# A decoder trunk in float32: the first feed-forward product by Strassen's seven, with stage pools that share bytes

## The chip, the cores and the metric

The kernel runs on one core of one Trainium2 chip. The metric is the device time of one execution in microseconds (us). Times of one kernel are given as a median of runs; a trace is one profiled execution.

## The reference

Two layers over x of 512 tokens by 1024 channels, all in float32. In each layer four causal token mixers read h = RMSNorm(x) @ W_in, and then:

```
mixed = sum_i sigmoid(gate_logits_i + b_gate_i) * (y_i @ W_branch_i)
x  <- x + mixed @ W_out
h2 = rms_norm(x, norm_ff)
x  <- x + square(relu(h2 @ W_ff1)) @ W_ff2
```

W_ff1 is 1024 x 4096 and W_ff2 is 4096 x 1024. A last RMSNorm ends it. The change concerns the part from `mixed @ W_out` on.

## The kernel before, in words

Activations lie transposed: tiles of 128 channels by 512 tokens, eight of them (x0 to x7) for x. Each float32 operand is split in two float32r tiles, a high part (a ScalarE copy) and the rest (a VectorE subtraction), and a product is made of three matmuls: high x high, low x high and high x low. Weights come in pieces of 128 x 1024 float32 (512 KB) from one array in the order of use. `chunk` (L265) issues the DMA of a piece (L271) from SyncE's queue into one of three buffers (wr0, wr1, wr2, a ring), copies the high part into a tile wh (L275, ScalarE) and leaves the low part in the buffer itself (L276, VectorE), so that a buffer is free only when the last matmul that reads its low part is done. `mtile` (L279) makes one tile of 128 output channels: 8 pieces of the contraction with 3 matmuls each, 24 of 128x512.

`layer` (L419) does the attention part as a list of steps written by hand, and ends it with the four branch products. Then come 8 tiles of w_out (L463), each added to x on VectorE; `norm_split` (L363) scales x by g and splits it into hh and hl; `rms` (L328) makes 1/rms by squares (ScalarE), additions (GpSimd, L339), a matmul with ones, a power (GpSimd) and a broadcast matmul. The feed-forward part has 4 groups: 8 tiles of w_ff1 (L472), each written out by max(0, .) * 1/rms (L475), squared (L476) and split (L478, L479), and 8 tiles of w_ff2 (L484), added to x (L485). `final` (L381) squares x, sums, and writes the scaled tiles out; the last w_ff2 tile is made in two halves of the tokens (`mhalves`, L291).

All tiles come from one pool `sb`, each tag with its own bytes for the whole program; the rings wr (3 of 1024 columns), yl and e (6 each of 512) are buffers laid out by hand. The Tile framework orders the instructions of each engine by priorities that the code sets (`high_priority`), and puts semaphore waits where a tile is read or its bytes reused. An engine takes its instructions strictly in that order, and so does SyncE's DMA queue.

## Time and profile before

| what | value |
|---|---|
| time, median of 3 runs | 2278.67 us (2275.55, 2278.67, 2278.78) |
| span of the profiled execution | 2273.7 us |
| median of the runs less that span | 5.0 us |
| TensorE busy | 98% of the span, 10740 matmuls, 10740 weight loads |
| VectorE, ScalarE, GpSimd busy | 65%, 46%, 19% |
| DMA | 204.75 MB, 90 GB/s on average |

The span goes from the first to the last record of the trace; the device time holds a little more at both ends. Busy is the sum of an engine's own instructions; the chain of waits goes back from the last instruction to what released it, step by step. "Granted clock" is the share of full speed that TensorE was given in a stretch: 1.00 is 2.4 GHz, 0.50 is 1.2 GHz.

### The profile page before, as it was taken

The page shows a single profiled execution, that of the slowest core. Times are in us where ns is not written, and L with a number is a line of the kernel's source. Part 1 is how long each engine was busy: PE and PEld are TensorE (multiplying, and loading weights), DVE is VectorE, ACT ScalarE, POOL GpSimd, SP SyncE. Part 2 cuts the span into 40 slices and gives each one's busy share as a digit, 9 for nine tenths or more (in the row PEclk, how much of TensorE's full clock was granted, in tenths as well). Part 3 has the DMA queues.
Part 4 walks back from the last instruction along what each step waited for, and adds up shares of the span by engine and source line. Part 5 has one row for each costly group of instructions (what it writes and reads, how often), then busy time and mean ns, then how long its engine had stood idle before and what let it go on. Part 6 is the DMA issues. An engine that isn't in the chain of part 4 may idle for free.

```text
span 2273.7 us, 28986 instructions
## 1 busy us (share of the span) xinstructions
PE 2230.2 (98%) x10740; PEld 1824.9 (80%) x10740; DVE 1488.2 (65%) x2434; ACT 1035.6 (46%) x1663; POOL 428.5 (19%) x759
## 2 busy tenths in 40 slices
PE   8999999999899999999999999999989999999998
PEld 7888878887788888888888888788868888888886
DVE  6889687888875444343458886978888654344344
ACT  5775544445544333232347654534454443232233
POOL 1223024434211200000112220234431112000000
PEclk9999999999999999999999999999999999999999
DMA  4222223322124332333432222233211243333332
GB/s 164 77 72 68 90 68 96 113 79 79 47 67 128 103 93 93 95 99 94 125 105 69 66 75 85 74 98 118 76 56 58 83 130 93 94 99 95 93 94 92
DMA packets 63108, 204.75 MB, mean 90 GB/s; under 512 B 7496, under 2 KB 10184, under 8 KB 62968
## 3 DMA queue, kind: packets, MB, share of 16 engines
q1 hardware_dynamic: 62968, 202.90, 29.1%
q8 instruction: 86, 1.41, 0.3%
q14 instruction: 54, 0.44, 0.1%
HBM read 198.57 MB, written 4.29 MB: 89 GB/s over the span
## 4 chain that ended last, share of the span: by engine, by line
PE 91%; DVE 5%; issue 1%; DMA 1%; ACT 1%; POOL 1%; POOLq 0%; DVEq 0%; SPq 0%; ACTq 0%
PE ps L121 48%; PE pd L121 42%; PE ps L730 1%; DMA wr1f<-in_w 0%; DMA wr0f<-in_w 0%; DVE sh L844 0%; POOL sm L613 0%; DVE wr1r L276 0%; DVE Q L616 0%; DVE m L1214 0%; DVE m L591 0%; DVE sx L609 0%; DVE m L605 0%; DVE Q L1109 0%; ACT wh L275 0%
## 5 line engine op out<-in xcount | busy, mean ns | idle before, releaser
L121 PE MATMUL pd<-hh,wh 128*128 128x512 f32 x1040 | 415.8, 400 | 0.2 <-ACT wh L275 0.2
L121 PE MATMUL pd<-hl,wh 128*128 128x512 f32 x1040 | 407.8, 392 | 0.0
L275 ACT ACTIVATE wh<-wr1f 128x1024 fp32r<-128x1024 f32 x112 | 118.7, 1060 | 274.7 <-PE ps L121 175.0
L275 ACT ACTIVATE wh<-wr0f 128x1024 fp32r<-128x1024 f32 x111 | 117.6, 1060 | 265.4 <-PE ps L121 176.3
L121 PEld LDWEIGHTS pd<-hh,wh 128*128 128x128 f32 x1040 | 195.6, 188 | 50.0 <-issue 4.0
L275 ACT ACTIVATE wh<-wr2f 128x1024 fp32r<-128x1024 f32 x111 | 117.6, 1060 | 256.9 <-PE ps L121 172.7
L121 PEld LDWEIGHTS pd<-hl,wh 128*128 128x128 f32 x1040 | 195.5, 188 | 42.2 <-issue 0.5
L121 PE MATMUL ps<-hh,wh 128*128 128x512 f32 x512 | 201.3, 394 | 0.0
L121 PE MATMUL ps<-hl,wh 128*128 128x512 f32 x512 | 199.3, 389 | 0.0
L276 DVE TENSOR_TENSOR wr0r<-wr0f,wh 128x1024 fp32r<-128x1024 f32 x111 | 143.4, 1292 | 43.0 <-ACT wh L275 42.5
L485 DVE TENSOR_TENSOR x<-x,ps 128x512 f32<-128x512 f32 (+1 forms) x65 | 44.2, 679 | 191.7 <-PE ps L121 191.7
L276 DVE TENSOR_TENSOR wr2r<-wr2f,wh 128x1024 fp32r<-128x1024 f32 x111 | 144.5, 1302 | 35.0 <-ACT wh L275 34.8
L121 PE MATMUL pd<-hh,wr2r 128*128 128x512 f32 x392 | 156.6, 400 | 0.0
L276 DVE TENSOR_TENSOR wr1r<-wr1f,wh 128x1024 fp32r<-128x1024 f32 x112 | 138.1, 1233 | 28.2 <-ACT wh L275 27.7
L475 DVE SCALAR_TENSOR_TENSOR p<-ps,rb 128x512 f32<-128x512 f32 x64 | 43.9, 691 | 157.3 <-PE ps L121 149.2
L121 PE MATMUL ps<-v,wh 128*128 128x512 f32 (+1 forms) x392 | 135.8, 389 | 0.0
L121 PE MATMUL pd<-hh,wr1r 128*128 128x512 f32 x336 | 134.4, 400 | 0.0
L121 PE MATMUL pd<-hh,wr0r 128*128 128x512 f32 x312 | 124.6, 399 | 0.0
L121 PE MATMUL ps<-p,v 128*128 128x384 f32 (+3 forms) x384 | 116.1, 426 | 2.2 <-POOL p L633 2.2
L121 PEld LDWEIGHTS ps<-hh,wh 128*128 128x128 f32 x512 | 96.1, 188 | 24.6 <-issue 0.5
L121 PE MATMUL pd<-yh,wh 128*128 128x512 f32 x256 | 105.0, 410 | 9.9 <-ACT yh L492 9.0
L121 PEld LDWEIGHTS ps<-hl,wh 128*128 128x128 f32 x512 | 96.2, 188 | 21.3
(638 smaller groups left out, 5326.8 us busy)
## 6 DMA issues: line engine op xcount, KB each, us to landing
wr0f<-in_w SPq DMA_DIRECT2D x117, 512.0 KB, 3.6
wr1f<-in_w SPq DMA_DIRECT2D x117, 512.0 KB, 3.6
wr2f<-in_w SPq DMA_DIRECT2D x116, 512.0 KB, 3.6
G<-gd SPq DMA_DIRECT2D x48, 128.0 KB, 3.1
x<-in_x SPq DMA_DIRECT2D x16, 256.0 KB, 3.5
xs<-x SPq DMA_DIRECT2D x8, 256.0 KB, 3.7
x<-xs SPq DMA_DIRECT2D x8, 256.0 KB, 3.3
out_y<-p SPq DMA_DIRECT2D x8, 256.0 KB, 2.4
```

Of the source, the lines that this page charges most:

```text
L121: i = self.nc.tensor.matmul(o, l, r, start=start, stop=stop, skip_group_check=True)
L275: nc.scalar.activation(wh[:], raw.f[:], AF.Copy)
L276: nc.vector.tensor_sub(raw[:], raw.f[:], fb(wh[:]))
L475: nc.vector.scalar_tensor_tensor(r[:], o[:], 0.0, self.rb[:], OP.max, OP.mult)
L485: nc.vector.tensor_add(x[m][:, h], x[m][:, h], o[:])
L730: nc.tensor.transpose(S3[n][:, c:c + P], at(F, q)[:, j * P:(j + 1) * P], self.ident)
```

## The change

The four groups of w_ff1 tiles become eight blocks of 512 hidden channels. For each, the 1024 x 512 piece of W_ff1 is seen as 2 x 2 quarters of 512 x 256, and x (scaled by g) as 2 x 2 quarters of 512 channels x 256 tokens. Winograd's form of Strassen's method makes the four quarter outputs of seven products instead of eight. `product` makes one of them with 24 matmuls of 128x256. The combinations of x (seven factors F11, F21, F22, F1 to F4, each high and low) are made once per layer in `factors`; those of the weights (s1 to s4) per block in `quarters`, by four VectorE additions of 128x1024 on the raw quarters; all seven weights of a block are split. Outputs are put together on the way out of PSUM: X, Y and Z are PSUM banks, `taken` copies one that goes on accumulating (e1, e2, e3). `finish` makes the last two products of a block, after product 11 of the next one. A w_ff2 group (`down`) stands after the blocks 2, 4 and 6 and at the end, there with `finish` between the two halves of its first two tiles' contraction.

The norm's scaling moves: the relu's and the square's results stay unscaled, x is multiplied by the mean square at the first block (8 VectorE multiplications) and by its reciprocal when the last w_ff2 group is added. `square_norm` makes both, so there are two broadcast matmuls per layer for one.

Storage: attention, feed-forward and end each open a pool of their own, and pools of different stages share bytes; a tile waits for the last reader of the bytes below it. In the feed-forward part the rings wr, yl and e together are nine buffers of 1024 columns (wr0 to wr2 and ww3 to ww8, of which ww3 to ww5 lie over yl and ww6 to ww8 over e), handed out by `take` in order of a list and given back by `drop`. wh has 5 buffers there instead of 2.

The core of the diff:

```
+    FF = dict(wh=(5, 1024), fx=(8, 1024), rl=(3, 1024), m=(2, 512), p=(6, 512), rt=(2, 4), ms=(2, 512))
+    END = dict(m=(1, 512), p=(4, 512), r=(3, 256), rt=(2, 4))
+    def stage(self, name, tags):
+        self.tags = tags
+        pool = self.tc.tile_pool(name=name, bufs=1, reuse_waits="tile")
...
+        nw = self.DUAL["wr"][0]
+        self.wfree = self.ring["wr"][1] + [pair("ww", i, 1024, start + i * 4096) for i in range(nw, total // 4096)]
+    def take(self):
+        b = self.wfree.pop(0)
...
+    def drop(self, d):
+        d.live = False
+        self.wfree.append(d.home)
...
             for l in range(self.depth):
-                x = self.layer(l, x)
-            self.final(x)
+                with self.stage(f"att{l}", self.ATT):
+                    self.mix(l, x)
+                with self.stage(f"ff{l}", self.FF):
+                    x = self.feed(l)
+            with self.stage("end", self.END):
+                self.final(x)
...
+        for m in OUT_ORDER:
+            wh, wl = self.chunk(wide=True)
+            o = self.ps("d")
+            self.halves(wh, wl, X2(HH), X2(HL), o[:], range(KT))
+            self.drop(wl)
...
+        for n in range(8):
+            W = self.quarters()
+            s = dict(W=W, X=self.ps("s"), H=hid)
+            self.product(s["X"], W["11"], F["11"], True)
+            s["e1"] = self.taken(s["X"])
+            if pend:
+                self.finish(pend, F)
+            if n > 0 and n % 2 == 0:
+                self.down(x, hid[:4], None)
+                del hid[:4]
+            if n == 0:
+                for k in range(KT):
+                    nc.vector.tensor_mul(x[k][:], x[k][:], ms[:])
+                s["Z"] = self.ps("s")
+                self.product(s["Z"], W["12"], F["21"], True)
+            s["Y"] = self.ps("s")
+            self.product(s["Y"], W["s3"], F["3"], True)
+            self.product(s["X"], W["s2"], F["2"], False)
+            s["e2"] = self.taken(s["X"])
...
+            self.product(s["X"], W["s1"], F["1"], False)
+            with self.evac():
+                e3 = self.taken(s["Y"])
+                nc.vector.tensor_add(s["rb"][:, S:], s["X"][:], e3[:])
+            pend = s
+        self.down(x, hid, rs, pend, F, l == self.depth - 1)
...
+    def product(self, o, W, F, start):
+        (wh, wl), (fh, fl) = W, F
+        for m in range(2):
+            d = o[:, m * 256:m * 256 + 256]
+            for k in range(4):
+                s = slice(k * 256 + m * P, k * 256 + m * P + P)
+                t = slice(k * 256, k * 256 + 256)
+                self.mm(d, wh[:, s], fh[:, t], start and m == 0 and k == 0, False)
+                self.mm(d, wl[:, s], fh[:, t], False, False)
+                self.mm(d, wh[:, s], fl[:, t], False, k == 3)
+        self.drop(wl)
+    def quarters(self):
+        with self.tc.high_priority(2000):
+            q = {}
+            for n in QUARTERS:
+                q[n] = self.take()
+                nc.sync.dma_start(q[n].f[:], self.A["w"][self.cidx])
+                self.cidx += 1
+            for d, a, b in (("s1", "21", "22"), ("s3", "21", "11"), ("s2", "s1", "11"), ("s4", "s2", "12")):
+                q[d] = q["21"] if d == "s3" else self.take()
+                nc.vector.tensor_add(q[d].f[:], q[a].f[:], q[b].f[:])
+            out = {}
+            for n in ("11", "s3", "s2", "12", "s1", "s4", "22"):
+                wh = self.t("wh", 1024, F32R)
+                nc.scalar.activation(wh[:], q[n].f[:], AF.Copy)
+                nc.vector.tensor_sub(q[n][:], q[n].f[:], fb(wh[:]))
...
+    def finish(self, s, F):
+        self.product(s["X"], W["s4"], F["22"], False)
+        with self.evac():
+            nc.scalar.activation(s["ra"][:, S:], s["X"][:], AF.Relu)
+            self.squares(s["ra"], s["H"], 1.0)
+        self.product(s["Y"], W["22"], F["4"], False)
+        with self.evac():
+            nc.vector.tensor_add(s["rb"][:, 0:S], s["Y"][:], s["e2"][:])
+            nc.scalar.activation(s["rb"][:], s["rb"][:], AF.Relu, scale=-1.0)
+            self.squares(s["rb"], s["H"], 1.0)
...
+                    nc.vector.tensor_add(x[m][:, h], x[m][:, h], o[:, 0:h.stop - h.start])
+                    if rs is not None:
+                        nc.vector.tensor_mul(x[m][:, h], x[m][:, h], rs[:, h])
...
+OUT_ORDER = (0, 1, 4, 5, 2, 3, 6, 7)
+QUARTERS = ("21", "22", "11", "12")
```

Three places show how the order moves. The first is SyncE's DMA queue in layer 0 around the end of the branches, before (line L271 is a weight, L160 a tile of x). The first w_out tile reads the wr1 of the fourth row, and the last branch tile the wr0 of the first.

```order
L271 DMA wr0f_55<-in_w 128x1024
L160 DMA x4_6601<-in_x 128x512
L160 DMA x5_6603<-in_x 128x512
L271 DMA wr1f_57<-in_w 128x1024
L271 DMA wr2f_59<-in_w 128x1024
L271 DMA wr0f_55<-in_w 128x1024
L160 DMA x6_6605<-in_x 128x512
L160 DMA x7_6607<-in_x 128x512
```

The same place now (L301 a weight, L577 a raw quarter, L190 a tile of x). The last branch tile reads the wr0 of the first row.

```order
L301 DMA wr0f_55<-in_w 128x1024
L301 DMA wr1f_57<-in_w 128x1024
L301 DMA wr2f_59<-in_w 128x1024
L301 DMA ww6f_91<-in_w 128x1024
L301 DMA ww7f_93<-in_w 128x1024
L301 DMA wr0f_55<-in_w 128x1024
L577 DMA ww8f_95<-in_w 128x1024
L190 DMA x0_6604<-in_x 128x512
```

The first w_out tile now takes the second wr0, of the sixth row, and the second and third tiles the wr1 and wr2 ahead of it; the seventh and eighth tiles take ww6 and ww7. All tiles of x stand behind them.

The second place is VectorE in layer 0 around the end of a w_ff2 group that is not the last, before: x6 and x7 are the last additions (L485), wr0r to wr2r low parts of weights (L276), L475 and L479 the work on a w_ff1 tile.

```order
L276 TENSOR_TENSOR wr1r_58<-wr1f_57,wh_1031_7934 128x1024
L485 TENSOR_TENSOR x6_6605<-x6_6605,ps_1030_7907 128x512
L276 TENSOR_TENSOR wr2r_60<-wr2f_59,wh_1033_7964 128x1024
L485 TENSOR_TENSOR x7_6607<-x7_6607,ps_1032_7937 128x512
L276 TENSOR_TENSOR wr0r_56<-wr0f_55,wh_1038_8000 128x1024
L475 SCALAR_TENSOR_TENSOR p_1035_7992<-ps_1034_7967,rb_931_6916 128x512
```

And now, after the first w_ff2 group: L709 are the additions to x, L581 the additions of quarters (s1, s3, s2 and s4 in this order), L673 that of the block before, L586 the low parts of the seven weights, L661 that of a squared tile.

```order
L709 TENSOR_TENSOR x6_6616<-x6_6616,pd_998_7668 128x512
L581 TENSOR_TENSOR wr2f_59<-ww7f_93,wr0f_55 128x1024
L709 TENSOR_TENSOR x7_6618<-x7_6618,pd_1000_7698 128x512
L581 TENSOR_TENSOR ww7f_93<-ww7f_93,ww3f_85 128x1024
L581 TENSOR_TENSOR ww6f_91<-wr2f_59,ww3f_85 128x1024
L673 TENSOR_TENSOR rl_1005_7801<-ps_1001_7724,p_1002_7773 128x512
L581 TENSOR_TENSOR ww4f_87<-ww6f_91,wr1f_57 128x1024
L586 TENSOR_TENSOR ww3r_86<-ww3f_85,wh_1007_7839 128x1024
L661 TENSOR_TENSOR fx_1017_7913<-rl_1004_7800,fx_1016_7912 128x1024
L586 TENSOR_TENSOR ww7r_94<-ww7f_93,wh_1008_7842 128x1024
```

Where one low part stood ahead of the next product, there are now three additions of quarters and one of the block before; ww3 holds the raw quarter "11", and its bytes are those of the last w_ff2 tile's weight (pd_1000).

The third place is ScalarE at the end, before: L388 are the squares of x0 to x6 for the last norm, L391 their scalings, L275 the weight copies of w_ff2 tiles.

```order
L275 ACTIVATE wh_2255_17777<-wr0f_55 128x1024
L388 ACTIVATE p_2264_17877<-x4_15429 128x512
L391 ACTIVATE x4_15429<-x4_15429,small_9008 128x512
L275 ACTIVATE wh_2257_17807<-wr1f_57 128x1024
L388 ACTIVATE p_2265_17881<-x5_15431 128x512
L391 ACTIVATE x5_15431<-x5_15431,small_9008 128x512
L388 ACTIVATE p_2266_17885<-x6_15433 128x512
L391 ACTIVATE x6_15433<-x6_15433,small_9008 128x512
L397 ACTIVATE r_2267_17889<-x7_15435 128x256
```

And now (L305 weight copies, L427 the square of half of x7, L418 the squares, L421 the scalings):

```order
L305 ACTIVATE wh_2295_19228<-wr2f_59 128x1024
L305 ACTIVATE wh_2297_19259<-ww3f_85 128x1024
L427 ACTIVATE r_2307_19347<-x7_16167 128x256
L418 ACTIVATE m_2300_19320<-x0_16153 128x512
L418 ACTIVATE p_2301_19323<-x1_16155 128x512
L418 ACTIVATE p_2302_19327<-x2_16157 128x512
L418 ACTIVATE p_2303_19331<-x3_16159 128x512
L418 ACTIVATE p_2304_19335<-x4_16161 128x512
L432 ACTIVATE x7_16167<-x7_16167,small_9744 128x256
L421 ACTIVATE x0_16153<-x0_16153,small_9744 128x512
```

All squares have moved behind the last weight copy and behind the square of x7's first half, which opens the end's pool.

## Rows read from the trace of the kernel before

**Rows 1.** The page, busy time of TensorE and its share of the span.

```profile
PE 2230.2 (98%) x10740; PEld 1824.9 (80%) x10740; DVE 1488.2 (65%) x2434; ACT 1035.6 (46%) x1663; POOL 428.5 (19%) x759
```

**Rows 2.** The chain of waits: shares by engine, then pieces (start us, us, what).

```profile
PE 91%; DVE 5%; issue 1%; DMA 1%; ACT 1%; POOL 1%; POOLq 0%; DVEq 0%; SPq 0%; ACTq 0%
...
671.86 64.25 PE pd L121 x278
736.10 52.73 PE ps L121 x228
...
798.22 344.80 PE ps L121 x1520
...
1150.07 11.07 PE ps L121 x94
```

**Rows 3.** Windows (busy us and count by engine, granted clock, DMA share, GB/s).

```profile
core 0: us, PE busy (x) PEld busy (x) DVE busy (x) ACT busy (x) POOL busy (x), PEclk, DMA share, GB/s
564.89:568.30 3.41, 3.41 (x10) 2.64 (x9) 3.41 (x15) 2.10 (x6) 2.88 (x6) 0.50 0.15 51
575.13:585.37 10.24, 7.32 (x24) 5.52 (x24) 9.40 (x15) 5.78 (x12) 3.89 (x4) 0.50 0.07 7
...
798.00:855.00 57.00, 57.00 (x249) 46.39 (x248) 26.09 (x31) 20.83 (x28) 0.00 (x0) 1.00 0.30 93
```

**Rows 4.** Timeline in w_ff1 (start us, us, engine line op): ScalarE's weight copies, one matmul.

```profile
804.49 1.06 ACT L275 ACTIVATE wh<-wr2f 128x1024 fp32r<-128x1024 f32 x1 [1.35 <-PE ps L121]
...
810.04 1.06 ACT L275 ACTIVATE wh<-wr0f 128x1024 fp32r<-128x1024 f32 x1 [3.30 <-PE ps L121]
...
826.68 1.06 ACT L275 ACTIVATE wh<-wr0f 128x1024 fp32r<-128x1024 f32 x1 [3.30 <-PE ps L121]
...
809.61 0.39 PE L121 MATMUL ps<-hl,wh 128*128 128x512 f32 x1
```

**Rows 5.** Timeline of TensorE at the start of layer 1: broadcast, then 256-column matmuls.

```profile
1149.05 1.02 PE L121 MATMUL pd<-m,cst 128*128 128x512 f32 x2
...
1150.03 0.28 PE L121 MATMUL ps<-wh,hh 128*128 128x256 f32 x1
```

**Rows 6.** Groups of instructions (busy us, mean ns of one, idle before).

```profile
L121 PEld LDWEIGHTS pd<-hh,wh 128*128 128x128 f32 x1040 | 195.6, 188 | 50.0 <-issue 4.0
...
L276 DVE TENSOR_TENSOR wr1r<-wr1f,wh 128x1024 fp32r<-128x1024 f32 x112 | 138.1, 1233 | 28.2 <-ACT wh L275 27.7
...
L485 DVE TENSOR_TENSOR x<-x,ps 128x512 f32<-128x512 f32 x63 | 43.3, 688 | 189.4 <-PE ps L121 189.4
...
L391 ACT ACTIVATE x<-x,small 128x512 f32<-128x512 f32 x7 | 5.1, 725 | 0.2
...
L388 ACT ACTIVATE p<-x 128x512 f32<-128x512 f32 x6 | 3.7, 618 | 3.9 <-DVE x L485 3.9
...
L339 POOL TENSOR_TENSOR m<-m,p 128x512 f32<-128x512 f32 x21 | 37.9, 1804 | 399.9 <-issue 313.9 <-ACT p L338 86.0
```

**Rows 7.** DMA issues of the page (KB each, median us from issue to landing).

```profile
wr0f<-in_w SPq DMA_DIRECT2D x117, 512.0 KB, 3.6
```

**Rows 8.** Timeline of TensorE ahead of and in a half-speed stretch of attention.

```profile
559.92 0.40 PE L121 MATMUL pd<-yl3r,wh 128*128 128x512 f32 x1
561.94 0.50 PE L121 MATMUL pd<-yh,wh 128*128 128x512 f32 x1 [1.62 <-ACT yh L492]
...
565.69 0.63 PE L121 MATMUL pd<-yh,wh 128*128 128x512 f32 x1
566.12 0.63 PE L121 MATMUL pd<-yh,wr2r 128*128 128x512 f32 x1
```

**Rows 9.** Timeline of the end.

```profile
2258.28 0.43 DVE L398 TENSOR_TENSOR r<-r,m 128x256 f32<-128x256 f32 x1 [0.48 <-ACT r L397]
...
2259.76 0.28 PE L121 MATMUL ps<-sh,wh 128*128 128x256 f32 x1
2259.88 0.50 PE L121 MATMUL pd<-cst,r 128*128 128x1 f32 x4
```

More of the change, by code (lines that the diff above doesn't have):

```diff
@@ L1 @@
+import contextlib
 import sys
@@ L269, in chunk @@
         with self.tc.high_priority(4000 if i == 0 else 2000):
-            raw = self.dual("wr")
+            raw = self.take() if wide else self.dual("wr")
             nc.sync.dma_start(raw.f[:], self.A["w"][i])
@@ new lines, in factors, with split @@
+    def factors(self, x, gcol):
+        nc = self.nc
+        F = {}
+        for n in ("11", "21", "22", "1", "2", "3", "4"):
+            F[n] = [self.st_pool.tile([P, 1024], F32R, name=f"F{n}{c}", tag=f"F{n}{c}", bufs=1) for c in "hl"]
+        v = lambda a: a.rearrange("p (k t) -> p k t", k=2)
+        for hf in range(2):
+            g = []
+            for k0 in (0, 4):
+                a = self.t("rl", 1024)
+                for i in range(2):
+                    k = k0 + hf * 2 + i
+                    nc.scalar.activation(a[:, i * S:i * S + S], x[k][:], AF.Copy, scale=gcol[:, k:k + 1])
+                g.append(v(a[:]))
+            b11, b12, b21, b22 = g[0][:, :, 0:256], g[0][:, :, 256:], g[1][:, :, 0:256], g[1][:, :, 256:]
+            def split(n, src):
+                fh, fl = (v(f[:, hf * S:hf * S + S]) for f in F[n])
+                nc.scalar.activation(fh, src, AF.Copy)
+                nc.vector.tensor_sub(fl, src, fb(fh))
+            split("11", b11)
+            split("21", b21)
+            split("22", b22)
+            t1, t2, t4 = (v(self.t("p")[:]) for _ in range(3))
+            nc.vector.tensor_sub(t1, b11, b12)
+            nc.vector.tensor_sub(b12, b22, b12)
+            split("3", b12)
+            nc.vector.scalar_tensor_tensor(t2, b22, -1.0, t1, OP.mult, OP.subtract)
+            split("2", t2)
+            split("1", t1)
+            nc.vector.scalar_tensor_tensor(t4, t2, -1.0, b21, OP.mult, OP.subtract)
+            split("4", t4)
+        return F
@@ new lines, in square_norm @@
+    def square_norm(self, x):
+        nc = self.nc
+        acc = self.t("m")
+        for k in range(KT):
+            if k == 0:
+                nc.scalar.activation(acc[:], x[k][:], AF.Square)
+            else:
+                sq = self.t("p")
+                nc.scalar.activation(sq[:], x[k][:], AF.Square)
+                nc.gpsimd.tensor_add(acc[:], acc[:], sq[:])
+        ss = self.ps("d")
+        for t in range(4):
+            self.mm(ss[:, t:t + 1], acc[:, t * P:(t + 1) * P], self.ones[:, 0:1], t == 0)
+        r, q = self.t("rt", 4), self.t("rt", 4)
+        nc.vector.tensor_scalar(r[:], ss[:, 0:4], 1.0 / D, EPS, OP.mult, OP.add)
+        nc.vector.reciprocal(q[:], r[:])
+        out = []
+        for c in (r, q):
+            dg = self.t("m")
+            nc.vector.tensor_tensor(dg[:].rearrange("p (a b) -> p a b", a=4),
+                                    self.ident.unsqueeze(1).to_broadcast([P, 4, P]),
+                                    c[:].unsqueeze(2).to_broadcast([P, 4, P]), OP.mult)
+            pb = self.ps("d")
+            self.mm(pb[:], self.ones, dg[:], True)
+            o = self.t("ms")
+            nc.scalar.activation(o[:], pb[:], AF.Copy)
+            out.append(o)
+        return out
@@ L1289, in weight_stream, with quarters @@
             f[it[0]](*it[1:])
-    for m in range(8):
+    for m in OUT_ORDER:
         out.append(_kxm(inp["w_out"][l], m * P))
-    for g in range(4):
-        for m in range(8):
-            out.append(_kxm(inp["w_ff1"][l], (g * 8 + m) * P))
-        for m in range(8):
-            out.append(_kxm(inp["w_ff2"][l][g * 1024:(g + 1) * 1024], m * P))
+    def quarters(n):
+        for q in QUARTERS:
+            i, j = int(q[0]) - 1, int(q[1]) - 1
+            c = n * 512 + i * 256
+            out.append(inp["w_ff1"][l][j * 512:(j + 1) * 512, c:c + 256].reshape(4, P, 256).transpose(1, 0, 2)
+                       .reshape(P, 1024))
+    for n in range(9):
+        if n < 8:
+            quarters(n)
+        if n > 0 and n % 2 == 0:
+            g = n // 2 - 1
+            for m in range(8):
+                out.append(_kxm(inp["w_ff2"][l][g * 1024:(g + 1) * 1024], m * P))
     return out
```

155 lines of the change are left out of this document (104 added, 51 removed).

## The prediction

> **What bounds the kernel now.** I read the page's busy shares first, then the chain of waits, the windows, and last the timelines of the places where the change moves something. TensorE is busy for 98% of the span [rows 1], and the chain that ended last is TensorE for 91%; in layer 0 it runs without a break from 671.86 through w_out (736.10) and from 798.22 for 344.80 us through both feed-forward products [rows 2]: each piece begins where the one before ends. In a window of w_ff1 TensorE is busy for 57.00 of 57.00 us at full granted clock, VectorE for 26 and ScalarE for 21 [rows 3]. So here time is TensorE's number of columns, and everything else is hidden. Two consequences: a saved matmul column is saved time, and any new wait of TensorE is lost time, since nothing stands beside it.
>
> **The gain.** In w_ff1 the ScalarE copies of weight tiles are each released by TensorE's progress; the one at 826.68 is the fourth after that at 804.49 [rows 4], 5.55 us a tile, 24 matmuls at 0.231 us. Of the matmuls with 256 columns at the start of layer 1 the chain holds 94 in a row that took 11.07 us, 0.1177 each [rows 2]. Each has its own weight load of 188 ns [rows 6], so the load is inside that pace. Per block of 512 channels: 4 tiles x 5.55 = 22.2 us before, 7 products x 24 x 0.1177 = 19.8 after. For 8 blocks and 2 layers, 355 less 316.4: **-38.5 us**. A rule of the Trainium skill speaks against this term: "TensorE: Matmul & The Clock Gate", The mechanism, says that a weight load overlaps matmuls in flight only when the row group differs, and its section LDWEIGHTS gives columns / 1.2 ns for one, so that every matmul would pay some 107 ns besides its columns (256 / 2.4 + 2.5 ns by the section Back-to-back issue gap); by it an estimate is 0.216 us for a 256-column matmul, 581 us for the products, and a sum 226 us above today's instead of 38.5 below. The rows just named disagree with it: 0.118 is all that one costs.
>
> w_ff2 keeps its 768 matmuls a layer, but reads its moving operand in two runs of 256. No row shows that: between nothing and the price of two starts for one, 2 x 0.1177 - 0.231 = 0.0044 us, 6.8 for both layers. I take nothing, since the columns are the same, and keep the 6.8 for the range. The second broadcast of the norm is one more ones-matmul in each layer; the one before had two passes that held TensorE for some 0.9 us (from 1149.05 to the next product's 1150.03) [rows 5]: **+1.8**.
>
> VectorE gets per block 7 subtractions and 4 additions of 128x1024 (1.23 us each [rows 6]), 3 additions of 128x512 (0.69) and 2 more subtractions: 18 us under 19.8 us of TensorE, and in the blocks with a w_ff2 group far less; ScalarE 7 copies at 1.06 and 6 smaller ones, 13 us. Both are covered on average. What is not covered are places where the last thing to arrive is a chain, and there the cover that I named is gone.
>
> **The stops that it adds.** A 512 KB weight lands 3.6 us after its issue [rows 7], and 0.43 us lie between the start of the last matmul before a wait and the start of the waiter (809.61, 810.04) [rows 4].
>
> *Branch end to w_out, both layers.* Before, the first w_out weight sat in the buffer that was next in the ring, freed two tiles earlier, and the chain shows no stop at 736.10. Now take() begins with wr0, which the last branch tile still reads: the DMA waits for its last-but-one matmul (layer 0; in layer 1 a wide buffer over the last e tiles). 0.43 + 3.6 + 0.4 behind two weights issued just ahead (estimate) + 1.06 copy, less 0.23 and the usual 0.3, then another 1.06 until the second tile's copy, which TensorE's order needs next: 6.3 in layer 0, 7.6 in layer 1. **+13.9** (11 to 15).
>
> *Entry of w_ff1.* After the last w_out addition VectorE has about 7.3 us of queue before the low part of factor 3 (two 1.23, seven 0.69); TensorE has products 11 and 21, 5.65 us: 1.8 late. Then product 2 waits for the ScalarE copy of e1, which stands behind seven squares whose buffers wait for GpSimd additions of 1.80 us [rows 6]: 1.3 to 2.5. Then 0.8 for s1. **+9** for both layers (3 to 12), and for smaller ones in the next two blocks **+3.2** (0 to 4).
>
> *After each of three inner w_ff2 groups per layer, six places.* The raw quarter "11" of the next block is loaded into the buffer of the last w_ff2 tile, so its DMA waits for that tile's last read. From there 0.43 + 3.6 until it has landed; then VectorE must add s3, s2 and s4, with one 0.69 for the previous block between them, and subtract: 4 x 1.23 + 0.69 = 5.6. Together 9.65 us until the third matmul of product 11. TensorE has left 2 x 0.231 + 35 x 0.118 + 2 x 0.118 = 4.8. So 4.9 us stand; in two of the six places the VectorE queue has one more subtraction ahead: 6.1. 4 x 4.9 + 2 x 6.1 = **+31.8**. Ends: 24 if the copy alone is waited for in some, 36 if the landing takes 4.3.
>
> *Last w_ff2 group of each layer.* The second half of the contraction needs the squares of the block just finished. From the last matmul of product s4 x F22: 0.43, relu 0.61, then ScalarE copy, square, copy, copy (two are weights), relu, square and copy at 1.06, and one VectorE subtraction of 1.23: 9.7 us, against 16 x 0.118 + 16 x 0.231 = 5.6 of TensorE's. **+8.1** (6 to 10).
>
> *Layer 0 to 1.* The low part of x0 stands on VectorE behind x7's addition and its new multiplication and two weight subtractions: 0.43 + 3 x 0.69 + 2 x 1.23 = 5.0, less 0.5 of work in hand; before, the chain shows no stop there. **+4.5** (3 to 5.5). The rest of layer 1's attention has nearly the old order; 0 to 4, taken as 0.
>
> *The end.* Before, the squares of x0 to x6 lay beside the last w_ff2 tiles, and x7's first half was summed at 2258.28, 1.5 us ahead of the last matmul (2259.76; its sum went to TensorE at 2259.88) [rows 9]. Now the end's tiles lie over bytes of the feed-forward stage and the first of them waits for the last matmul. Then ScalarE: seven squares at 0.62, four scalings at 0.73 that stand between them [rows 6], two half ops, 8.2 us in all, then two additions: the sum is ready 9.7 us after the last matmul instead of 0.1. **+9.6** (7 to 11).
>
> *The granted clock.* In the attention part TensorE stood for 1.6 us at 559.92 to 561.94 and 0.9 soon after; from 564.89 it ran for 3.41 us at 0.50, the 1.2 GHz level, where 512-column matmuls start 0.43 us apart (565.69, 566.12) [rows 3, 8]. There are 10.2 us at 0.50 from 575.13, after longer gaps. In w_ff1's window it is 1.00 [rows 3]. The eleven new stops of 4 us and more are longer than those; each is likely to be followed by a half-speed stretch such as the first: 3.41 x (1 - 0.231/0.43) = 1.6 us. Some fall while TensorE stands anyway: **+12** (3 to 22).
>
> **The sum.** -38.5 + 1.8 + 13.9 + 9 + 3.2 + 31.8 + 8.1 + 4.5 + 9.6 + 12 = +55.4. The profiled execution has a span of 2273.7 us; the median of the three runs, 2278.67, is 5.0 above it, which I take as what lies around the span. 2273.7 + 5.0 + 55.4 = **2334 us**, 2.4% slower. With all low ends +20 (2299), with all high ends, those of attention and the two runs with them, +90 (2369); they will not all fall on one side.
>
> **Rivals.** *The waits aren't there* (faster side): if the weights land in time at the branch end and after the inner groups, because what waits there is further back than I read, the 45.7 us of those two terms and most of the clock's 12 go. Then -2.3, 2276; with the other terms at their low ends -18, 2261. The point from which it decides: the stops together must stay under 36.7 us. For it speaks that a weight lands in two thirds of a w_ff2 tile's time and that the DMA share is 0.30 [rows 3]; against it that each of those DMAs waits for a read that is a few matmuls before the product that needs it. Faster 0.06, within 0.2% (4.6 us, about what a measurement of this kernel can tell from no change) 0.04.
>
> *The clock does more.* If each of the eleven stops brings 10.24 us at 0.50, as at 575.13, a stop costs 10.24 x 0.46 = 4.7: 52 instead of 12, 2374. For it: one of the two such stretches shown is long [rows 3]. Against: those hold many short matmuls and more gaps; behind the new stops TensorE works without a break. 0.07.
>
> *A product goes at the pace of weight loads*, 0.188 instead of 0.118: 2688 x 0.07 = 188 more, 2522. For it: a load is as long as that in every row [rows 6]. Against: the measured pace, loads and all [rows 2]. 0.01.
>
> *Forecast*, the stops as summed: 0.82. It and the last two are slower: 0.90. The range 2301 to 2360 leaves out the faster rivals, the clock's, and a little of the forecast's own ends.
>
> **What would show it.** In the changed profile: w_ff1 matmuls 0.118 us apart with the clock at 1.00; TensorE's share below 96%; in each layer stops of 5 to 8 us ahead of the first w_out tile, with the release from a ScalarE weight copy, of about 5 us after the second, fourth and sixth block's w_ff2 group with a wr or ww buffer as releaser, and of 4 in the last group; GpSimd's square additions ahead of product 2; about 10 us more between the last w_ff2 matmul and the end; short runs of 0.50 clock behind stops in the feed-forward part. I am wrong if TensorE still runs without breaks there, or if the products start later than 0.12 us apart.

## The result, and the profile after

The changed kernel takes **2347.8 us** (median of 4 runs, 2341.24 to 2349.51); the kernel before, on the same chip, 2277.1 (4 runs, 2273.81 to 2278.78). The ratio is 1.0309, with a 95% interval of 1.0293 to 1.0325: 3.1% slower. The forecast was 2334, slower, with a range of 2301 to 2360: the sign and the range held, and the time came out 13.8 us above the forecast. The profiled execution has a span of 2345.6 us, against 2273.7: 71.9 us more to explain.

The page of the changed kernel, its lines on TensorE, the chain of waits and the weights' DMA:

```profile
PE 2234.7 (95%) x11896; PEld 1883.2 (80%) x11896; DVE 1645.8 (70%) x2563; ACT 1142.9 (49%) x1773; POOL 429.9 (18%) x757
...
PE 86%; DVE 7%; DMA 2%; ACT 2%; issue 2%; POOL 1%; SPq 0%; POOLq 0%; DVEq 0%; ACTq 0%
...
wr0f<-in_w SPq DMA_DIRECT2D x92, 512.0 KB, 3.3
```

TensorE's share falls from 98% [rows 1] to 95%, and its part of the chain from 91% [rows 2] to 86%. Its busy time doesn't fall, although there are fewer columns: for one thing, busy time counts half-speed stretches at their full length, and there are many more of them now.

**The gain is there.** The timeline of TensorE in a product (start us, us, engine line op):

```profile
855.05 0.28 PE L147 MATMUL ps<-F1h,ww4r 128*128 128x256 f32 x1
855.16 0.28 PE L147 MATMUL ps<-F1l,wh 128*128 128x256 f32 x1
855.28 0.28 PE L147 MATMUL ps<-F1h,wh 128*128 128x256 f32 x1
855.40 0.28 PE L147 MATMUL ps<-F1h,ww4r 128*128 128x256 f32 x1
```

The starts are 0.117 us apart, as in the 94 matmuls of [rows 2]. Each has its own weight load (the page counts 11896 of both), so the load costs nothing beside the columns here. The Trainium skill ("TensorE: Matmul & The Clock Gate", The mechanism) says that a weight load overlaps matmuls in flight only when the row group differs. For these loads of the full array the trace disagrees.

**The stops are there too.** TensorE's timeline, layer 0 and the end; in brackets how long it stood idle and what released it:

```profile
745.28 0.79 PE L147 MATMUL pd<-fx,wh 128*128 128x512 f32 x1 [5.22 <-ACT wh L305]
...
796.97 0.39 PE L147 MATMUL ps<-F21l,wh 128*128 128x256 f32 x1 [0.45 <-DVE F21l L610]
799.91 0.38 PE L147 MATMUL ps<-F3l,wh 128*128 128x256 f32 x1 [0.53 <-DVE F3l L610]
805.61 0.58 PE L147 MATMUL ps<-F2h,wh 128*128 128x256 f32 x1 [3.54 <-ACT p L554]
811.77 0.39 PE L147 MATMUL ps<-F1h,wh 128*128 128x256 f32 x1 [0.63 <-ACT p L554]
...
909.77 0.57 PE L147 MATMUL ps<-F3h,wh 128*128 128x256 f32 x1 [1.51 <-ACT wh L585]
911.82 0.58 PE L147 MATMUL ps<-F11h,ww3r 128*128 128x256 f32 x1 [1.48 <-DVE ww3r L586]
...
1123.19 0.50 PE L147 MATMUL pd<-fx,wh 128*128 128x512 f32 x1 [2.58 <-ACT fx L660]
...
1168.92 0.38 PE L147 MATMUL ps<-wh,hl 128*128 128x256 f32 x1 [4.20 <-DVE hl L401]
...
2330.15 1.01 PE L147 MATMUL pd<-cst,r 128*128 128x1 f32 x4 [8.10 <-DVE r L428]
```

In order: the first w_out tile, four stops at the entry of w_ff1, the products after the first w_ff2 group (two stops), the last group's second half, the start of layer 1, the end. Each stands where the prediction put it. How the chain behind such a stop looks, at the first inner group (SyncE's queue, then VectorE):

```profile
903.41 0.33 SPq L577 DMA_DIRECT2D ww3f<-in_w  x1
...
906.54 1.23 DVE L581 TENSOR_TENSOR ww7f<-ww7f,ww3f 128x1024 f32<-128x1024 f32 x1 [2.21 <-DMA ww3f<-in_w]
907.68 1.22 DVE L581 TENSOR_TENSOR ww6f<-wr2f,ww3f 128x1024 f32<-128x1024 f32 x1
908.82 0.68 DVE L673 TENSOR_TENSOR rl<-ps,p 128x512 f32<-128x512 f32 x1
909.42 1.21 DVE L581 TENSOR_TENSOR ww4f<-ww6f,wr1f 128x1024 f32<-128x1024 f32 x1
910.55 1.22 DVE L586 TENSOR_TENSOR ww3r<-ww3f,wh 128x1024 fp32r<-128x1024 f32 x1
```

Quarter 11 is issued at 903.41 and lands 3.1 us later; three sums and one 0.68 stand ahead of its low part (910.55), which releases TensorE at 911.82, as forecast. The stop just before it (909.77) is one that the forecast doesn't name: TensorE's order has the first matmul of product s3 there, and it waits for ScalarE's copy of that sum.

**The clock.** Windows of the changed kernel (busy us and count by engine, granted clock, DMA share, GB/s): one over the first w_ff2 group and the products ahead of it, then stretches behind stops, and one in attention:

```profile
854.00:907.00 53.00, 52.54 (x262) 43.94 (x261) 17.90 (x20) 10.20 (x13) 0.00 (x0) 1.00 0.25 83
...
742.55:749.38 6.83, 3.94 (x8) 2.84 (x9) 5.90 (x7) 5.21 (x6) 0.03 (x1) 0.50 0.74 277
803.99:810.82 6.83, 5.21 (x24) 5.21 (x25) 3.62 (x3) 2.58 (x4) 6.52 (x5) 0.50 0.00 0
...
909.81:916.64 6.83, 5.35 (x23) 5.06 (x24) 6.83 (x7) 5.81 (x6) 0.00 (x0) 0.50 0.10 40
1090.71:1097.54 6.83, 4.74 (x20) 4.44 (x21) 6.79 (x7) 6.49 (x7) 0.00 (x0) 0.50 0.08 32
...
1124.85:1128.26 3.41, 3.41 (x9) 2.63 (x9) 1.23 (x1) 1.39 (x2) 0.00 (x0) 0.50 0.00 0
...
575.30:592.37 17.07, 13.34 (x53) 11.33 (x53) 15.83 (x23) 7.71 (x15) 7.46 (x7) 0.50 0.09 31
```

Behind nearly every place where TensorE stood for some 3 us and more it runs at 0.50, the 1.2 GHz level, for 3.41 or 6.83 us. Before, there was no such stretch between 585 and 1687 us; now there are six from 742 to 1128, one at 1169.22, and six from w_out of layer 1 on, thirteen in all.

### Where the 71.9 us are

A stop is the distance of two starts less the usual one (0.231 or 0.118); the clock's cost is what matmuls inside a half-speed stretch take beyond those. Where a distance holds both, the split between them is good to about 1 us in a row of the table.

| term | forecast | measured |
|---|---|---|
| products instead of tiles, second broadcast | -36.7 | pace as forecast |
| branch end to w_out, two layers | +13.9 | 14.1 |
| entry of w_ff1, two layers | +9 | 11.5 |
| smaller ones in the next blocks | +3.2 | 2.8 |
| six inner w_ff2 groups | +31.8 | 27.9 |
| last w_ff2 group, two layers | +8.1 | 6.1 |
| layer 0 to 1 | +4.5 | 4.4 |
| the end | +9.6 | 9.9 |
| granted clock behind these stops | +12 | 22.9 |
| attention | 0 | 5.8 |
| sum | 55.4 | 68.7 of 71.9 |

The attention's 5.8 are 3.95 in layer 0 (the last branch matmul starts at 739.66 for 735.71) and 1.8 in layer 1. The first matmul of layer 1 and its last branch matmul, before and then in the changed kernel:

```profile
1136.61 0.28 PE L121 MATMUL ps<-wh,hh 128*128 128x256 f32 x1
1858.85 0.39 PE L121 MATMUL pd<-e3r,wh 128*128 128x512 f32 x1
...
1164.32 0.40 PE L147 MATMUL ps<-wh,hh 128*128 128x256 f32 x2
1894.26 0.40 PE L147 MATMUL pd<-e5r,wh 128*128 128x512 f32 x1
```

That is 722.2 us before and 729.9 now: 7.7 more, of which the stop at its start takes 4.4 and the half-speed stretch behind that 1.5. The 3.2 us that the sum leaves lie in the two feed-forward parts, which took 50.4 us more than before from the last branch matmul to the last w_ff2 matmul; their rows above come to 47.1.

### The profile page after: what moved, and what is told of

It reads as the page before. It is cut to its first block, busy times and chain, and to the rows that moved or that the text cites. A ratio compares the mean times of both kernels' runs of the same rounds, so it can differ in the third digit from the quotient of the medians.

```text
span 2345.6 us, 31548 instructions
## 1 busy us (share of the span) xinstructions
PE 2234.7 (95%) x11896; PEld 1883.2 (80%) x11896; DVE 1645.8 (70%) x2563; ACT 1142.9 (49%) x1773; POOL 429.9 (18%) x757
## 4 chain that ended last, share of the span: by engine, by line
PE 86%; DVE 7%; DMA 2%; ACT 2%; issue 2%; POOL 1%; SPq 0%; POOLq 0%; DVEq 0%; ACTq 0%
PE pd L147 60%; PE ps L147 25%; PE ps L958 1%; DMA wr0f<-in_w 1%; ACT wh L305 0%; DVE wr1r L306 0%; DVE wr2r L306 0%; DMA ww4f<-in_w 0%; POOL sm L841 0%; DMA ww8f<-in_w 0%; DVE wr0r L306 0%; DVE Q L1337 0%; POOL m L635 0%; DVE sh L1072 0%; DVE Q L844 0%
## 5 line engine op out<-in xcount | busy, mean ns | idle before, releaser
L147 PE MATMUL pd<-fx,wh 128*128 128x512 f32 (+1 forms) x1296 | 408.6, 394 | 18.5 <-ACT wh L305 13.0
L147 PEld LDWEIGHTS pd<-fx,wh 128*128 128x128 f32 x1296 | 245.5, 190 | 77.4 <-ACT wh L305 14.9
L305 ACT ACTIVATE wh<-wr0f 128x1024 fp32r<-128x1024 f32 x77 | 81.6, 1059 | 160.4 <-PE pd L147 93.5
L709 DVE TENSOR_TENSOR x<-x,pd 128x512 f32<-128x512 f32 (+1 forms) x65 | 44.1, 679 | 144.2 <-PE pd L147 143.7
L305 ACT ACTIVATE wh<-wr1f 128x1024 fp32r<-128x1024 f32 x68 | 72.0, 1059 | 112.7 <-PE pd L147 93.4
L305 ACT ACTIVATE wh<-wr2f 128x1024 fp32r<-128x1024 f32 x70 | 74.1, 1058 | 98.7 <-PE pd L147 82.0
L861 POOL TENSOR_SCALAR_AFFINE_SELECT p<-p 128x128 f32<-128x128 f32 x192 | 81.9, 447 | 161.5 <-ACT p L860 159.9
L764 POOL TENSOR_TENSOR mixed<-mixed,gt 128x512 f32<-128x512 f32 x48 | 65.4, 1366 | 248.7 <-DVE gt L762 247.5
L306 DVE TENSOR_TENSOR wr2r<-wr2f,wh 128x1024 fp32r<-128x1024 f32 x70 | 94.6, 1351 | 13.8 <-ACT wh L305 13.5
L409 DVE SCALAR_TENSOR_TENSOR gt<-pd,rb 128x512 f32<-128x512 f32 x64 | 43.9, 686 | 77.6 <-PE pd L147 77.5
L147 PEld LDWEIGHTS ps<-p,v 128*128 128x128 f32 x384 | 70.0, 190 | 34.3 <-issue 9.7
L841 POOL COPY sm<-sx 32x16 f32<-32x16 f32 x192 | 52.0, 271 | 221.3 <-DVE sx L837 205.8
```

What stands on the lines that cost most here:

```text
L147: i = self.nc.tensor.matmul(o, l, r, start=start, stop=stop, skip_group_check=True)
L305: nc.scalar.activation(wh[:], raw.f[:], AF.Copy)
L306: nc.vector.tensor_sub(raw[:], raw.f[:], fb(wh[:]))
L409: self.nc.vector.scalar_tensor_tensor(dst, o, scale, self.rb[0:o.shape[0], :], OP.mult, OP.mult)
L709: nc.vector.tensor_add(x[m][:, h], x[m][:, h], o[:, 0:h.stop - h.start])
L764: nc.gpsimd.tensor_add(self.mixed[m][:], self.mixed[m][:], g)
```

## Experiments

Theory, as at the prediction: each stop has the cause that its term names, and with a stop its half-speed stretch goes. Rivals: another operand of the same product is as late, so that a stop only moves; or the shared pools cost by themselves. Medians are of 4 runs; "before" is the kernel before on the same chip, which took between 2275.2 and 2278.3, so 2 to 3 us of a difference to the changed kernel's 2347.8 can lie with the chip. All but one kernel change the changed kernel.

### The weights of w_out

`a_order` hands out buffers at the start of w_out that were read longest ago:

```
+        r, ww = self.ring["wr"], sorted((b for b in self.wfree if b not in self.ring["wr"][1]), key=lambda b: b[0].name)
+        i = r[0] % 3
+        self.wfree = [r[1][i], r[1][(i + 1) % 3]] + ww[0:3] + [r[1][(i + 2) % 3]] + ww[3:]
         for m in OUT_ORDER:
```

> Only the order in which the feed-forward part takes its wide buffers is changed: the two wr buffers that were freed first, then ww3 to ww5, then the wr that the last branch tile reads, then the rest. Theory of the waits (the stop ahead of w_out is the late DMA): the stops of 5.4 + 0.5 us in layer 0 and 7.7 + 0.5 in layer 1 and the half-speed stretches behind them (1.6 and 1.7 us of excess) go: 17.4 us less than the changed kernel, 2330. Rival (the copies and low parts of mixed, which now wait for attention's bytes, come just as late): under 5 us less, the stop ahead of w_out stays with a VectorE or ScalarE copy of mixed as releaser.

2348.8 us (2348.43 to 2349.61), 1.0316 of before (1.0299 to 1.0334): no gain. ScalarE and TensorE there:

```profile
737.87 1.06 ACT L305 ACTIVATE wh<-wr1f 128x1024 fp32r<-128x1024 f32 x1 [2.22 <-PE pd L147]
...
742.62 2.69 ACT L499 ACTIVATE fx<-mixed 128x512 fp32r<-128x512 f32 x5
...
743.29 0.80 PE L147 MATMUL pd<-fx,wh 128*128 128x512 f32 x1 [5.45 <-ACT fx L499]
```

The same engine in the changed kernel:

```profile
737.78 2.17 ACT L499 ACTIVATE fx<-mixed 128x512 fp32r<-128x512 f32 x4
744.17 1.06 ACT L305 ACTIVATE wh<-wr0f 128x1024 fp32r<-128x1024 f32 x1 [4.22 <-DMA wr0f<-in_w]
```

There the copies of mixed came first and the weight last, released by its DMA. With the edit the weight has landed, yet its copy waits for TensorE's last branch matmul, because the wh buffers of the new pool lie over bytes that attention reads until then. Four more weight copies follow, and only then the copies of mixed, which w_out reads too. So the forecast's chain is right for that kernel, and a second chain of nearly the same length stands behind it: the DMA was sufficient for the stop, but not necessary. That the shared bytes hold the copy back is read from its releaser here; s_stages, below, shows the same wait with the old DMA order.

`aw_order_pool` adds wh buffers that no other stage's tiles share: five in the pool of the whole program, and so five for attention instead of two.

```
-    ATT = dict(wh=(2, 1024), yh=(5, 512), ...
+    ATT = dict(wh=(5, 1024), yh=(5, 512), ...
+        pool = self.sb if tag == "wh" else self.st_pool
```

> As a_order, and the high parts of weights (wh, 5 buffers) come from a pool of the whole program, so that the first copies of w_out needn't wait for the last branch matmul that reads the bytes below. In a_order the weights had landed, but the copy of the first stood until that matmul was done, four more weight copies followed, and then the eight copies of mixed. Theory (two causes in a row, the DMA and the shared bytes of wh): the stops at both w_out starts (5.6 and 1.2 in a_order, in either layer) fall under 1.5: 14 to 17 us less than the changed kernel, 2331 to 2334. Rival (the copies of mixed wait for attention's bytes themselves): 4 us or more are left at each w_out start, with a copy of mixed as releaser.

2387.4 us (2382.49 to 2391.1), 1.0492 (1.0476 to 1.0508). The first w_out stop of layer 0 shrinks to 3.1 us and a second of some 1.8 follows; but attention, whose order of work the five buffers change, takes until 761.6 in layer 0 for 739.7, and 751 us for 730 in layer 1. The run tells nothing on the price of w_out. It shows how far this kernel's order hangs on a count of buffers.

### The inner w_ff2 groups

`c_quarter` loads quarter 11 first and puts its low part into a tile of its own (lo), so that product 11 waits for no sum:

```
+            wh, lo = self.t("wh", 1024, F32R), self.t("lo", 1024, F32R)
+            nc.scalar.activation(wh[:], q["11"].f[:], AF.Copy)
+            nc.vector.tensor_sub(lo[:], q["11"].f[:], fb(wh[:]))
+            out["11"] = wh, lo
...
-QUARTERS = ("21", "22", "11", "12")
+QUARTERS = ("11", "21", "22", "12")
```

> The raw quarter 11 is loaded first of the four, so it lies in the buffer of the sixth w_ff2 tile and not of the eighth, and its low part goes to a tile of its own, so that it need not wait for the sums s3 and s2. Theory of the waits: the six stops after inner w_ff2 groups (27.9 us by the trace of the changed kernel) and the half-speed stretches behind them (10.5) go: 38 us less, 2309. Rival (VectorE's queue after a w_ff2 group is the limit, so that the stop moves to product s3 or s2): 10 to 20 us less, with TensorE standing at F3 or F2 in the same six places. Rival on the clock (256-column products lower the granted clock by themselves): half-speed stretches stay in these six places.

2331.0 us (2327.96 to 2332.76), 1.0236 (1.022 to 1.0251): 16.8 less than the changed kernel, of the 38.5 that stops and clock cost at these places. In the profiled executions the two feed-forward parts are 5.2 and 6.1 us shorter, and 5.7 more come from layer 0's attention, whose code is the same: that is scatter and no gain of the edit. TensorE after the first inner group:

```profile
908.16 0.38 PE L147 MATMUL ps<-F3h,wh 128*128 128x256 f32 x1 [1.31 <-ACT wh L591]
910.05 0.38 PE L147 MATMUL ps<-F2h,wh 128*128 128x256 f32 x1 [1.51 <-ACT wh L591]
```

The stop has gone from product 11 to the next ones, s3 and s2, whose sums are now the late ones: 2.7 to 3.7 us for 4.0 to 5.5. The rival was right here.

`q_s3_early` follows that: s3 is made next, in 11's buffer, with a tile lo of its own, and s2 as s3 + 22, which is the same sum.

```
+            for n in ("11", "s3"):
+                if n == "s3":
+                    nc.vector.tensor_add(q["11"].f[:], q["11"].f[:], q["21"].f[:])
...
+            for d, a, b in (("s2", "11", "22"), ("s1", "21", "22"), ("s4", "s2", "12")):
```

> As c_quarter, and s3 is added into the buffer of quarter 11 (its low part, too, goes to a tile of its own), s2 is made as s3 + 22, so that s3 needs only the two quarters that land before the group's end. In c_quarter TensorE stood at F3 and F2 for 1.5 to 1.8 us each, waiting for ScalarE copies behind VectorE's sums, which wait for quarter 22, the last to land. Theory (the last quarter to land sets the stop): at F3 nothing is late, at F2 there are 2.8 us more of TensorE's work in hand: the six stops fall from 27.9 to under 6, with their half-speed stretches: 30 to 38 us less than the changed kernel, 2310 to 2318. Rival (ScalarE and VectorE queues of that place are full, 5 copies and 8 operations): no better than c_quarter, 2331.

2309.2 us (2305.74 to 2311.39), 1.0148 (1.0131 to 1.0164): **38.6 less**. The window that holds the stops of 909.77 and 911.82 in the changed kernel, and the last group:

```profile
908.00:925.00 17.00, 17.00 (x147) 17.00 (x146) 15.51 (x16) 13.41 (x17) 0.00 (x0) 1.00 0.30 93
...
1104.21 0.79 PE L147 MATMUL pd<-fx,wh 128*128 128x512 f32 x1 [4.82 <-ACT fx L669]
```

TensorE is busy for 17.00 of 17.00 us, at full clock: all six stops are gone, and all six half-speed stretches with them. The six stops measured 27.9 us and their stretches 10.6 (2.1, 1.3, 1.9, 2.0, 1.9 and 1.3), together 38.5, and the run gave back 38.6. That the two agree so well is in part luck: the last group's stop has grown from 2.7 to 5.0 us in layer 0, so part of what was saved is waited for there, while layer 0's attention happened to end 1.9 us earlier and the two stretches at the entry of w_ff1 were 3.41 us long for 6.83. The two feed-forward parts are 16.7 and 20.3 us shorter. This is the test of the clock's term: the same 256-column products run at full clock once the stops are gone, so the products themselves don't lower it.

### The last group

`e_three` puts three first halves instead of two ahead of the last two products:

```
-        for m in range(2):
+        for m in range(3):
...
-            if m < 2:
+            if m < 3:
```

> Three tiles of each w_ff2 group, not two, have the first half of their contraction ahead of the last block's two products (the third in a bank of the s tag). Theory: 12 more matmuls of 0.231, 2.8 us, stand beside the chain of squares in the last group, so its stop falls from 3.2 to under 0.7, and its half-speed stretch (1.5) goes: 6 to 8 us less than the changed kernel over both layers, 2340 to 2342. Rival (the third tile's weight copy delays the squares on ScalarE by 1.06): the stop falls only by 1.7, 3 us less in all.

2390.7 us (2381.7 to 2391.5), 1.0499 (1.0479 to 1.0518): 43 us more, and the theory fell. The stop that it aimed at is still 2.5 us. In every inner group new stops of 1.0 to 2.4 us stand instead; two of them:

```profile
845.49 0.58 PE L147 MATMUL ps<-F2h,wh 128*128 128x256 f32 x1 [2.24 <-ACT p L554]
...
855.05 0.50 PE L147 MATMUL pd<-fx,wh 128*128 128x512 f32 x1 [1.15 <-ACT wh L305]
```

The edit keeps three weights with their wh tiles in use in all groups, of five wh, and a bank of another tag with them. The releasers, a copy of an output and a copy of a weight, fit that; no run gave it a wh or a bank more, so the cause isn't shown.

### The norm at the entry

`b_norm` moves the norm's squares, and the eight multiplications, behind the first block:

```
-        ms, rs = self.square_norm(x)
...
             pend = s
+            if n == 0:
+                ms, rs = self.square_norm(x)
+                for k in range(KT):
+                    nc.vector.tensor_mul(x[k][:], x[k][:], ms[:])
```

> The norm's squares, additions and broadcasts and the multiplication of x are emitted after the first block's last product instead of before its first. Theory (the copies of PSUM banks share the p tiles with the squares, which wait for GpSimd's additions): the stop of 3.7 us at product 2 of the first block of each layer and the half-speed stretch behind it (2.3) go, the two smaller ones of VectorE's queue (0.6 and 0.7) stay: 12 us less, 2336. Rival (VectorE and ScalarE are full at the entry whatever they do first): under 4 us less, the stop moves to another product of the first two blocks.

2347.0 us (2341.16 to 2349.81), 1.0304 (1.0283 to 1.0324): the same as the changed kernel. First the changed kernel, GpSimd and ScalarE at the stop of 805.61:

```profile
798.23 15.56 POOL L635 TENSOR_TENSOR m<-m,p 128x512 f32<-128x512 f32 x7 [55.66 <-ACT p L634]
...
802.24 1.15 ACT L634 ACTIVATE p<-x 128x512 f32<-128x512 f32 x2 [1.05 <-POOL m L635]
804.44 0.63 ACT L634 ACTIVATE p<-x 128x512 f32<-128x512 f32 x1 [1.05 <-POOL m L635]
804.98 0.58 ACT L554 ACTIVATE p<-ps 128x512 f32<-128x512 f32 x1
```

The copy of e1 (804.98) stands on ScalarE behind squares that wait for GpSimd's additions, as forecast. The squares wait in turn for the additions: the first of the seven took 3.97 us and the next 2.12, for 1.80 in [rows 6]. With the edit that stop of 3.7 us is gone, and a new one of 2.8 begins at 819.6, ahead of the norm's own broadcast, while the first inner group's stop is larger:

```profile
909.34 0.38 PE L147 MATMUL ps<-F11h,wh 128*128 128x256 f32 x1 [1.77 <-ACT wh L586]
912.18 0.38 PE L147 MATMUL ps<-F3h,wh 128*128 128x256 f32 x1 [2.46 <-ACT wh L586]
```

The cause is right and the edit still gives nothing: the same squares, additions and multiplications now stand ahead of other waiters. The rival again.

### The end

`t_end` makes the last norm in the last feed-forward pool:

```
-            with self.stage("end", self.END):
-                self.final(x)
+                    if l == self.depth - 1:
+                        self.final(x)
...
-                sq = self.t("r", 256)
+                sq = self.t("rl", 256)
```

> The last norm takes its tiles from the last feed-forward pool instead of a pool over the same bytes. Theory: the squares of x0 to x6 stand beside the last w_ff2 tiles again; from the last w_ff2 matmul to the end 14 us instead of 23.8: 9.9 us less, 2338. Rival (the final multiplication of x by 1/mean square, new on VectorE, is what makes the end late): under 4 us less.

2337.4 us (2335.73 to 2339.76), 1.0266 (1.0251 to 1.0281): 10.4 less. TensorE at the end:

```profile
2319.96 0.28 PE L147 MATMUL pd<-fx,wh 128*128 128x256 f32 x1
2320.08 0.50 PE L147 MATMUL pd<-cst,rl 128*128 128x1 f32 x4
```

The last norm's matmul follows the last product at once, as before [rows 9], and from the last w_ff2 matmul to the end there are 13.97 us, for 23.78 in the changed kernel and 13.91 before. Opening a pool was the whole term.

### Sharing without Strassen

`s_stages` is the kernel **before**, with its tiles in a pool for each attention, feed-forward and end stage and nothing else changed in its computation:

```
+                with self.stage(f"att{l}"):
+                    self.layer(l, x)
+                with self.stage(f"ff{l}"):
+                    x = self.feed(l)
+            with self.stage("end"):
+                self.final(x)
```

> The kernel before, with w_ff1 as it was, but attention, feed-forward and end in pools that share bytes (all tags as they were, 2048 bytes of DMA scratch). Theory (part of the change's cost is the sharing): the end is 23.8 us long instead of 13.9, the first copies of w_out wait for the last branch matmul (4 to 6 us in each layer, 1.6 of half speed behind each), and layer 1 begins 2 to 4 us late: 20 to 28 us more than before, 2298 to 2306. Rival (the sharing costs only at the end): 10 us more, 2288.

2309.3 us (2308.84 to 2310.07), before 2275.2 (2273.09 to 2276.32), 1.015 (1.0135 to 1.0166): **34 us more**, above what was expected. ScalarE and TensorE at the first w_out tile of layer 0, and TensorE at the start of layer 1:

```profile
739.49 1.06 ACT L289 ACTIVATE wh<-wr1f 128x1024 fp32r<-128x1024 f32 x1 [2.22 <-PE pd L131]
...
741.40 2.18 ACT L475 ACTIVATE v<-mixed 128x512 fp32r<-128x512 f32 x4
...
742.06 0.50 PE L131 MATMUL ps<-v,wh 128*128 128x512 f32 x1 [2.61 <-ACT v L475]
...
1148.43 0.52 PE L131 MATMUL ps<-wh,hh 128*128 128x256 f32 x2 [1.76 <-ACT hh L384]
1150.39 0.58 PE L131 MATMUL ps<-wh,hl 128*128 128x256 f32 x1 [1.44 <-DVE hl L385]
```

The first weight copy waits for the last branch matmul (739.05), and all copies of mixed stand behind it on ScalarE; before, the first had begun at 735.52, ahead of that matmul (735.71). At the start of layer 1 the first tiles of hh and hl are late in the same manner. From the last w_ff2 matmul to the end there are 23.3 us, as in the changed kernel. Layer 1's attention takes 729.3 us for 722.2, 4.2 of the 7 us at its start. So sharing alone loses 34 us, about half of what the changed kernel loses; 3.3 of them lie in layer 0's attention (last branch matmul at 739.05 for 735.71), which is within the scatter of that part.

### All that helped, together

`qtf_all` has the edits of q_s3_early and t_end, and the last block's two products ahead of the first halves of the last group:

```
+        if pend:
+            self.finish(pend, F)
         for m in range(2):
             W.append(self.chunk(wide=True))
...
-        if pend:
-            self.finish(pend, F)
```

> The edits of c_quarter and q_s3_early (quarter 11 first, its low part in a tile of its own, s3 made in 11's buffer) and of t_end (the last norm in the last feed-forward pool) together, and one more: the last two products of the eighth block stand ahead of the two first halves of the last w_ff2 group instead of behind them, so that 24 matmuls of 512 columns, 5.5 us, lie between product 22 and the first matmul that reads its squares. Theory (each stop has its own cause, so what the edits gave adds up, and the 5.5 us cover most of the last group's stop of 5.0 us in q_s3_early): 2347.8 - 38.6 - 10.4 - 2 x 2.7 = 2293, between 2287 and 2298, with no half-speed stretch in the feed-forward part behind the inner groups and an end of 14 us. Rival 1 (the stop of the last group stays, since ScalarE's queue of weight copies and not the number of matmuls between sets it): 2298 to 2301, the stop still 4 to 5 us. Rival 2 (with the stops gone, another wait takes their place, as in b_norm): above 2303. By none of them is it as fast as before (2277).

2287.2 us (2284.27 to 2288.29), before 2276.4 (2273.55 to 2277.64), 1.0053 (1.0036 to 1.007): 60.6 less than the changed kernel, and still slower than before. TensorE at w_out and at the last group of layer 0:

```profile
739.87 0.80 PE L147 MATMUL pd<-fx,wh 128*128 128x512 f32 x1 [5.95 <-ACT wh L305]
...
1094.79 0.50 PE L147 MATMUL pd<-fx,wh 128*128 128x512 f32 x1 [1.83 <-ACT fx L669]
```

The last group's stop falls from 5.0 to 2.0 us. The gains add up (38.6 + 10.4 + 2 x 3.0 = 55), and the rest lies in layer 0's attention, whose last branch matmul starts at 733.52 for 739.66. That rest is scatter: without it the run would lie at the theory's 2293. What is left of the loss: stops of 6.1 and 5.6 us at the two w_out, of 3.7 at each entry of w_ff1, of 2.0 in each last group, of 2.9 and 1.4 at the start of layer 1, and the clock behind them.

## Why the prediction was right, and where its sizes were off

**What bounds the kernel and the gain: right.** With TensorE at 98% the saved columns and the new waits went through to the end, and the products have the pace that 94 matmuls at the start of layer 1 had shown. (The sum's own figures give 38.6, not 38.5.)

**The stops: right by place, and near by size.** The seven terms of waits, without clock and attention, came to 76.7 for a forecast of 80.1. c_quarter and q_s3_early show that quarter 11's chain was the cause in the inner groups (the stops moved when it alone was shortened, and went when s3's was too), t_end shows the end's. The inner groups were over-sized (27.9 for 31.8), in part since a weight lands 3.1 us after its issue at the place shown and 3.3 in the page's median, not 3.6 [rows 7]. The entry of w_ff1 was under-sized (11.5 for 9): VectorE's part is 1.3 us a layer and not 1.8, and the wait for the squares 3.7 and not 1.3 to 2.5, with GpSimd's first two additions at 3.97 and 2.12 us and not 1.80. For w_out the total was right and the cause incomplete: the pieces written down for layer 0 add up to 6.0 and not to 6.3, layer 1's 7.6 has no working, and measured are 5.9 and 8.2. The late DMA that I named was one of two chains of about equal length in layer 0, and a_order, which takes it away, gained nothing of the 17.4 us that it was expected to give.

**The clock: the term that was mis-sized.** I took 1.6 us a stop, from the one stretch of 3.41 us in [rows 3, 8], and 12 in all; measured are 22.9, about the term's upper end of 22. Of the thirteen stretches eight are 6.83 us long and cost 1.6 to 2.4 each, and five are 3.41 long and cost 1.3 to 1.6. Two of the thirteen, at the entry of w_ff1, follow stops that the term didn't count; they cost 4.6. The other eleven cost 18.3, or 1.7 each, so the price of 1.6 a stop was right, although the length behind it often wasn't: much of a longer stretch falls where TensorE stands. The step that failed is "Some fall while TensorE stands anyway", which took eleven times 1.6, 17.6, down to 12, and the count of eleven. Some of this is scatter: in t_end the stop at the entry of layer 0 has the same 3.7 us, and the stretch behind it is 3.41 us long and costs 1.2 for 2.3.

**Attention: taken as 0, with an end of 4 for layer 1; it was 5.8.** Layer 1's 1.8 lies within that end. Layer 0's 3.95 stands in no term: the step that failed is the silent one that attention of the same code takes the same time. That part is mostly scatter: its code is the same in the changed kernel and in a_order, c_quarter, t_end, b_norm, e_three, q_s3_early and qtf_all, and there the last branch matmul starts between 733.52 and 739.66 (735.71 before); half-speed stretches make much of it, as the one of 17.07 us from 575.30, which before was 10.24 [rows 3]. Layer 1's isn't: from its start to the last branch matmul it takes 727.5 to 731.4 us in the changed kernel and in these seven, and 729.3 in s_stages, for 722.2 before. Which of its waits make up the part beyond the stop at its start and the stretch behind that, some 2 us, the runs leave open.

The two misses, 10.9 and 5.8, less 3.4 for the over-sized waits, are 13.3 of the 16.5 us by which the span (2345.6) came out above the forecast's 2273.7 + 55.4. The medians differ by less, 13.8, since the median of the runs is 2.2 us above the span now, for 5.0 before. Those 5.0 are not what lies around the span, as I took it: a run's time is 1.7 us above its own span (2347.26 and 2345.6), and the rest was the difference of two runs.

**The rivals.** That the waits aren't there fell with TensorE's timeline. That the clock does more has a part of the truth in the length, eight stretches being twice as long as the forecast's, and little in the price: 1.7 us a stop and not 4.7.

## What to carry to other kernels

Where one engine is busy for 98%, an algorithm with fewer operations is worth no more than its weakest hand-over: count the places where its operands are made just in time, and price each as the wait plus what the clock takes behind it. Price the means apart from the end: the pools that had to share bytes to make room cost 34 us without the algorithm, nearly the 38.5 that it saves. And when a stop goes, look at once for the next operand that the same engine needs: in three of the edits here (a_order, c_quarter, b_norm) all or part of a stop only moved to the next one that waits.

## What the runs showed of the hardware that I hadn't expected

- The half-speed stretches measured 3.41, 6.83, 10.24 and 17.07 us, and the length of the stop alone doesn't set that of the stretch. Behind the stop of 3.7 us at the entry of w_ff1 in layer 0 it was 6.83 in the changed kernel and 3.41 in a_order, t_end and q_s3_early. Behind the stop of 2.7 us in layer 0's last group it was 3.41 in the changed kernel and t_end, and a_order has none there.
- GpSimd's seven additions at the entry of w_ff1 took 15.56 us, one after the other, for 1.80 each in the mean before [rows 6]: the first 3.97, then 2.12 to 2.15, two of 1.28, and 2.15, in both layers alike. VectorE and ScalarE are busier beside them now, which may be the cause of the longer ones but wasn't tried; why two are shorter is open.
- Layer 0's attention, from the same code, ended within a spread of 6 us from kernel to kernel, so a difference of some us between two kernels' times needs the trace before it is put down to an edit.
